# A decoder block's hand-ordered middle stretch rewritten: projection's second half to the FFN's second round

## The chip, the core and the metric

The kernel runs on one core of one Trainium2 chip. The metric is the device time of one execution in microseconds (us), and the number compared is the median of several runs. PE is TensorE (matmul), DVE is VectorE, ACT is ScalarE, POOL is GpSimd, SP is SyncE. In this kernel SP issues the loads and POOL issues the stores of intermediate results.

## What is computed

One layer of a decoder block on a sequence of 1024 tokens, width D = 1024, all in float32. A mixer (a gated convolution and a stick-breaking attention, merged) is projected back by `w_o`, normalised, gated and added to x. Then comes a SwiGLU feed-forward network (FFN) of inner width D_FF = 2816, with RMSNorm before and after and shift, scale and gate from the conditioning vector c:

```python
def swiglu_ffn(h, w_ffn_in, w_ffn_out):
    gate, up = jnp.split(h @ w_ffn_in, 2, axis=-1)
    return (jax.nn.silu(gate) * up) @ w_ffn_out
...
        h = rmsnorm(x, pre_mix_g[l]) * (1.0 + sc1) + sh1
        y = hybrid_mixer(h, w_in[l], conv_w[l], ...)        # ends in merged @ w_o
        x = x + ga1 * rmsnorm(y, post_mix_g[l])
        h = rmsnorm(x, pre_ffn_g[l]) * (1.0 + sc2) + sh2
        y = swiglu_ffn(h, w_ffn_in[l], w_ffn_out[l])
        x = x + ga2 * rmsnorm(y, post_ffn_g[l])
```

The change lies between `merged @ w_o` and the first rounds of `h @ w_ffn_in`.

## The kernel before, in words

**Layout.** Channels lie on the 128 partitions, tokens run along the free axis in two halves c = 0 and c = 1 of 512. A float32 product is made of three fp32r passes: each operand is split into `hi` (a copy rounded to fp32r, on ACT) and `lo` (the difference, on DVE), and PE adds hi·hi, hi·lo and lo·hi in one PSUM bank. One matmul is 128x512 by 128x128. A weight tile of 128x1024 is loaded as `raw` and then split (`load_w`); raw, hi and lo have three buffers each in the pool `wp`.

**Projection.** `merged @ w_o` makes eight output tiles of 128 channels for each token half, 24 matmuls each (8 input tiles, 3 passes). The second half (c = 1) is `step(k)`, in the order `WORDER`. Three of its weights are still in their buffers from the first half; five are loaded and split again. `evac` copies a bank out on ACT, squares it on ACT and adds the square into `ysum` on DVE. `total` sums `ysum` over channels with a matmul by `ones` in plain fp32 (banks `psq`, `psx`). `res` multiplies by the root from that sum, adds x and squares the sum on ACT; a second total (`psx`) gives the pre-FFN norm, and `scaled` applies it: a DVE multiply by the root, then ACT's scale and shift.

**FFN, first matmul.** It runs in 22 rounds f, one per block of 128 gate and 128 up channels. Each round computes its four half-blocks (gate and up, two token halves) with a scheme of seven products instead of eight, each of 4 x 3 = 12 matmuls. The operands on the token side are B11, B21 (parts of the first token half), T1 to T4 (sums of parts of both halves) and B22. The weight side of a round needs the sums s1 to s4 and the parts a11, a12 and a22. The products accumulate in the banks `ka`, `kc` and `kb`. The first two products of a round need only the first token half, so for the first `EARLY` = 9 rounds they are done ahead (`ke(f, 0)` and `ke(f, 1)`, with weight `early_w(f)`), beside the second half's norms. Each goes to a bank of its own; ACT copies the first out (`e_first`), DVE adds the second to it (`e_second`), and both results are stored to DRAM in `e_d` and loaded again in round f. So a round f < EARLY has 60 matmuls and a later one 84.

**FFN, second matmul.** Its weight is used in the same scheme. `w2_forms(j)` makes its sums during rounds 9 to 19 (`W2_AT`, which follows `EARLY`), 4 stores of 512 KB each into `w_d`. The gated results go to `g_d` through POOL and are loaded as X and Y. `gb11_0` is the first operand of this matmul, made on ACT from X.

**Order.** `pin(begin)` fixes the order in which instructions stand on PE, DVE and ACT from `begin` (before `step(0)`) to the last early product, as the code is written. Everything else, and all of SP and POOL, is ordered by the scheduler. An instruction waits for its inputs and for a free buffer, and all behind it on its engine wait with it. The lines that matter most:

```python
        def early_w(f):
            wes[f] = load_w(w1[f], f"we{f}", act, dve)
...
        for j in (2, 3):
            los.append(operand("T2", j, t2s[j]))
        early_w(6)
        ke(5, 0)
        ke(5, 1)
```

## Time and profile before

| | |
|---|---|
| median of 3 runs | 1459.28 us (1458.99 to 1460.12) |
| the profiled execution's own time | 1457.92 us |
| its span, first to last instruction | 1456.1 us |
| PE busy | 1389.9 us (95% of the span) |
| DVE busy | 1021.7 us (70%) |
| ACT busy | 658.6 us (45%) |
| mean granted TensorE clock | 0.993 |

The median is what a change is measured by. The rows further down come from the profiled execution, whose span lies 1.8 us below its own time. Busy shares are averages over stages with different limits, so what an edit is worth is read from the stage that it touches. In a list of waits each row names the engine and the tile that it wrote, whom it waited for, the sum, the number of waits and the longest.

### The profile page before, as it was taken

Reading aid. Unit: us, or ns where it says so; the run is one execution under the profiler, and the core shown is the slowest. Engines: PE = TensorE matmul, PEld = TensorE weight load, DVE = VectorE, ACT = ScalarE, POOL = GpSimd, SP = SyncE. Lnnn points to the kernel's source line nnn. Section 1 sums busy time; section 2 is a strip of 40 time slices with the busy share of each in tenths; the row PEclk is TensorE's granted clock in tenths of the full one; section 3 lists DMA queues with packets and bytes.
Section 4 is the critical chain, followed back from the end, with each engine's and each line's share of the span. In section 5 each row is a group of like instructions: output and inputs, shape, how many; then the busy total and the mean of one; then the engine's idle time right before and its main releaser. Section 6 shows DMA issues by size and latency. Waiting matters only on the chain.

```text
span 1456.1 us, 18905 instructions
## 1 busy us (share of the span) xinstructions
PE 1389.9 (95%) x6888; PEld 1162.5 (80%) x6888; DVE 1021.7 (70%) x1503; ACT 658.6 (45%) x1143; POOL 193.2 (13%) x275
## 2 busy tenths in 40 slices
PE   5999999999999999999989899999999997999996
...
GB/s 380 84 44 68 122 44 145 50 61 95 44 131 117 248 141 206 274 249 143 284 116 149 126 180 163 134 174 252 254 253 246 253 191 358 116 318 296 285 120 116
DMA packets 89932, 255.84 MB, mean 176 GB/s; under 512 B 9584, under 2 KB 19952, under 8 KB 88816
## 3 DMA queue, kind: packets, MB, share of 16 engines
...
## 4 chain that ended last, share of the span: by engine, by line
issue 46%; PE 43%; POOL 6%; DMA 2%; DVE 2%; ACT 1%; POOLq 0%; SPq 0%; DVEq 0%; ACTq 0%
PE ka L1222 8%; PE pb L1222 4%; PE pg L179 3%; PE pgv L179 3%; PE pv L381 3%; PE pcv L361 3%; PE pgg L179 2%; PE pq L179 2%; PE pk L179 2%; PE pa L1222 2%; PE tr L471 2%; POOL w_d L106 2%; POOL g_d L106 2%; PE av L481 1%; PE av L480 1%
## 5 line engine op out<-in xcount | busy, mean ns | idle before, releaser
L461 POOL TENSOR_TENSOR be<-be,ka 128x127 f32<-128x127 f32 (+2 forms) x96 | 99.8, 1053 | 233.7 <-DVE ka L459 118.5
L459 DVE TENSOR_TENSOR_SCAN ka<-ka 128x128 f32<-128x128 f32 (+2 forms) x96 | 95.2, 1015 | 40.1 <-ACT ka L455 40.0
L475 DVE TENSOR_TENSOR alo<-tr,ahi 128x512 fp32r<-128x512 f32 x80 | 53.3, 684 | 44.2 <-ACT ahi L474 43.7
L455 ACT ACTIVATE ka<-z 128x128 f32<-128x128 f32 (+2 forms) x96 | 47.7, 498 | 54.9 <-PE z L454 36.3
L474 ACT ACTIVATE ahi<-tr 128x512 fp32r<-128x512 f32 x80 | 46.5, 603 | 44.9 <-PE tr L471 32.5
L1222 PE MATMUL ka<-gt,w2f 128*128 128x512 f32 x264 | 63.1, 389 | 0.0
L1222 PEld LDWEIGHTS ka<-gt,w2f 128*128 128x128 f32 x264 | 49.6, 188 | 10.3
L790 PE MATMUL pwo<-mhi,wo_hi 128*128 128x512 f32 x128 | 51.0, 398 | 3.4 <-ACT wo_hi L158 1.7
L955 PE MATMUL ke<-b,we_hi 128*128 128x512 f32 x144 | 47.8, 414 | 5.3 <-ACT we_hi L158 5.3
L134 DVE SCALAR_TENSOR_TENSOR ada<-ada,cb 128x1024 f32<-128x1024 f32 x32 | 39.0, 1222 | 17.5 <-DMA ada<-in_ada_dram 17.3
L790 PE MATMUL pwo<-mhi,wo_lo 128*128 128x512 f32 x128 | 50.0, 390 | 0.5 <-DVE wo_lo L168 0.5
L456 ACT ACTIVATE be<-z 128x128 f32<-128x128 f32 (+2 forms) x96 | 47.4, 502 | 6.0 <-PE tr L471 5.9
L790 PE MATMUL pwo<-mlo,wo_hi 128*128 128x512 f32 x128 | 50.0, 390 | 0.1
L471 PE MATMUL tr<-ident,be 128*128 128x128 f32 x288 | 49.2, 273 | 0.7 <-DVE alo L475 0.4
L480 PE MATMUL av<-ahi,vst 128*128 128x256 f32 x160 | 44.6, 293 | 2.0 <-ACT be L456 1.2
L481 PE MATMUL av<-alo,vst 128*128 128x256 f32 x160 | 43.2, 296 | 2.1 <-DVE alo L475 1.9
L106 POOL DMA_DIRECT2D g_d<-uw x22 | 11.9, 543 | 246.2 <-DVE uw L1175 246.2
L361 PE MATMUL pcv<-ph,cvw 128*128 128x128 f32 x320 | 42.8, 276 | 1.3 <-DMA ph<-v_d 1.3
L361 PEld LDWEIGHTS pcv<-ph,cvw 128*128 128x128 f32 x320 | 39.7, 192 | 2.1 <-DMA ph<-v_d 1.1
L1103 PE MATMUL kb<-b,a 128*128 128x512 f32 x156 | 40.9, 389 | 0.0
L1222 PE MATMUL ka<-gb,wa 128*128 128x512 f32 x132 | 33.2, 400 | 7.9 <-ACT gb L158 7.9
L1103 PE MATMUL ka<-b,a 128*128 128x512 f32 x156 | 39.7, 389 | 0.0
(512 smaller groups left out, 4075.6 us busy)
## 6 DMA issues: line engine op xcount, KB each, us to landing
...
w2r<-in_w_dram SPq DMA_DIRECT2D x44, 256.0 KB, 3.8
...
```

Of the source, the lines that this page charges most:

```text
L106: nc.gpsimd.dma_start(dst, src)
L179: pe.matmul(bank, st[:, cols], mv[k][:, c * CH:(c + 1) * CH], start=(i == 0 and s == 0), stop=(i == n - 1 and s == 2))
L361: pe.matmul(cv[:, gi * TM:(gi + 1) * TM], wts[n][:, at:at + P], ph[:, g, SH - 1 - d:SH - 1 - d + TM], start=(d == 0), stop=(d == SH - 1))
L459: dve.tensor_tensor_scan(rev, rev, rev, init, op0=ALU.mult, op1=ALU.bypass)
L461: pool.tensor_tensor(beta[:, :m], beta[:, :m], kap[:, s_lo + 1:s_lo + 1 + m], op=ALU.mult)
L471: pe.transpose(tr[:, o:o + P], src, ident)
L475: dve.tensor_tensor(alo, tr, ahi, op=ALU.subtract)
L480: pe.matmul(avc, lhs, ahi[:, cols], start=(jp == c and jj == 0), stop=False)
L481: pe.matmul(avc, lhs, alo[:, cols], start=False, stop=(jp == 0 and jj == 1))
L790: pe.matmul(bank_, st[:, cols], mv[k][:, cs], start=(k == 0 and q == 0), stop=(k == KT - 1 and q == 2))
L1103: pe.matmul(bank_, st[:, cols], t[:, mv], start=(first and j == 0 and s == 0), stop=(j == HK - 1 and s == 2), skip_group_check=not first)
L1222: pe.matmul(dst, w[st][:, cols], g[mv], start=first and s == 0, stop=last and s == 2, skip_group_check=more)
```

## The change

It rewrites the hand order from the projection's second half on and lets it run on through rounds 0 and 1 of the FFN (`PIN = 2`). For this, `ffn(f)` is a generator that yields between its products, so that the hand order can put other instructions between them. `evac` is cut into its ACT and its DVE part, `load_w` into load (`wl`), hi (`wh`) and lo (`wlo`), and a root into its ACT part and a function for its DVE part. EARLY goes from 9 to 11. Both early products of a block accumulate in one bank; ACT copies it out after the first and after the second, and DVE adds nothing. They are done in twos: `ke(4,0)`, `ke(5,0)`, `ke(4,1)`, `ke(5,1)`. The norm is one DVE operation (times scale, times root), and the shift is added where hi and lo are made, or in the sums T1 to T4. psx1 sums five tiles instead of eight. The sums of round 0 have three tiles of their own.

```diff
-EARLY = 9
+EARLY = 11
...
-        def scaled(c, n, r):
-            y = h2[n, c]
-            dve.tensor_tensor(y, y, r, op=ALU.mult)
-            act.activation(y, y, AF.Identity, bias=mod[:, 24 + n:25 + n], scale=scale2[:, n:n + 1])
...
-        def make_b(n, eng):
-            t, y = B_AT[n], h2[n, 0]
-            copy_to(eng, t[:, 0], y)
-            dve.tensor_tensor(t[:, 1], y, t[:, 0], op=ALU.subtract)
...
-        def e_first(f):
-            es[f] = wtmp(f"e0_{f}")
-            act.activation(es[f], kbs[f, 0], AF.Copy)
-            store(e_d[f][:, 0], es[f])
-
-        def e_second(f):
-            e1 = wtmp(f"e1_{f}")
-            dve.tensor_tensor(e1, kbs[f, 1], es[f], op=ALU.add)
-            store(e_d[f][:, 1], e1)
-
-        def t2_sub(j):
-            b11, b12, b22 = h2[j, 0], h2[j, 1], h2[HK + j, 1]
-            dve.tensor_tensor(b11, b12, b11, op=ALU.subtract)
-            t2 = t2s[j] = wtmp(f"t2_{j}")
-            dve.tensor_tensor(t2, b22, b11, op=ALU.subtract)
...
+        def norm(c, n, r):
+            y = h2[n, c]
+            dve.scalar_tensor_tensor(y, y, scale2[:, n:n + 1], r, op0=ALU.mult, op1=ALU.mult)
+
+        def shift(n):
+            return mod[:, 24 + n:25 + n]
+
+        def bh(t, n, c):
+            act.activation(t[:, 0], h2[n, c], AF.Identity, bias=shift(n), scale=1.0)
+
+        def bl(t, n, c):
+            dve.scalar_tensor_tensor(t[:, 1], h2[n, c], shift(n), t[:, 0], op0=ALU.add, op1=ALU.subtract)
...
+        def ke(f, i):
+            if i == 0:
+                kbs[f] = dbank(f"ke{f}")
...
+                    pe.matmul(kbs[f], wes[f][st][:, cols], t[:, mv], start=(i == 0 and j == 0 and q == 0),
+                              stop=(j == HK - 1 and q == 2), skip_group_check=i > 0)
+
+        def e(f, i):
+            t = wtmp(f"e{i}_{f}")
+            act.activation(t, kbs[f], AF.Copy)
+            store(e_d[f][:, i], t)
...
+        def t12(j):
+            b11, b12, b22 = h2[j, 0], h2[j, 1], h2[HK + j, 1]
+            dve.tensor_tensor(b11, b12, b11, op=ALU.subtract)
+            T2[j] = wtmp(f"t2_{j}")
+            dve.scalar_tensor_tensor(T2[j], b22, shift(HK + j), b11, op0=ALU.add, op1=ALU.subtract)
+            hi_of("T2", j, T2[j])
...
+        for i, t in enumerate((xsum, xs(1, 2), xs(1, 6), xs(1, 3), xs(1, 7))):
+            pe.matmul(psx, ones, t, start=i == 0, stop=i == 4)
...
+        s0 = [po_.tile([P, CH], F32, tag="wt", name=f"s0_{i}", bufs=3) for i in range(3)]
+        for t, src in zip(s0, (w1[0][:, :CH], w1[FT][:, :CH], w1[FT][:, CH:])):
+            load(t, src)
...
+        for _ in r1:
+            pass
+        pin(begin)
+
+        for f in range(PIN, FT):
+            raw_w(f)
+            for _ in ffn(f):
+                pass
```

Three places show how instructions move. In the rows an arrow points from what is read to what is written.

The first place is ACT in the projection's second half. Squares of the residual sum are `xr0_*<-y0_*`; `y1_*<-pwo1_*` and `ysq1_*<-pwo1_*` are the copy and the square of an output tile; `wo1_3_hi` and `wo1_2_hi` are hi halves of the fifth and sixth weight. Before:

```order
L827 ACTIVATE xr0_4_6366<-y0_0_6199 128x512
L827 ACTIVATE xr0_4_6366<-y0_1_6234 128x512
L798 ACTIVATE y1_2_6608<-pwo1_6_6536,gpost1_159 128x512
L804 ACTIVATE ysq1_6_6610<-pwo1_6_6536 128x512
L827 ACTIVATE xr0_6_6369<-y0_2_6276 128x512
L827 ACTIVATE xr0_6_6369<-y0_3_6318 128x512
L158 ACTIVATE wo1_3_hi_6623<-wo1_3_raw_6621 128x1024
L798 ACTIVATE y1_3_6655<-pwo1_7_6583,gpost1_159 128x512
L804 ACTIVATE ysq1_7_6657<-pwo1_7_6583 128x512
L158 ACTIVATE wo1_2_hi_6667<-wo1_2_raw_6665 128x1024
```

After, where `w_o4_hi` and `w_o5_hi` are the hi halves of the same two weights and `L834` has the squares:

```order
L834 ACTIVATE xr0_2_6365<-y0_2_6278 128x512
L798 ACTIVATE y1_2_6590<-pwo1_1_6565,gpost1_159 128x512
L804 ACTIVATE ysq1_6_6592<-pwo1_1_6565 128x512
L158 ACTIVATE w_o4_hi_6594<-w_o4_raw_6499 128x1024
L834 ACTIVATE xr0_2_6365<-y0_3_6320 128x512
L834 ACTIVATE xr0_4_6368<-y0_0_6201 128x512
L834 ACTIVATE xr0_4_6368<-y0_1_6236 128x512
L798 ACTIVATE y1_3_6641<-pwo1_2_6616,gpost1_159 128x512
L804 ACTIVATE ysq1_7_6643<-pwo1_2_6616 128x512
L158 ACTIVATE w_o5_hi_6645<-w_o5_raw_6501 128x1024
```

Before, all eight squares of the residual, up to `xr0_6`, stand ahead of the fifth weight's hi; after, three of them do (`xr0_0` twice, `xr0_2` once), the next three follow it, and `xr0_6` comes behind the sixth.

The second place is ACT around the seventh early weight (`we6_hi` before, `w_6_hi` after). `L840` is the scale and shift of the second token half, `T2_*o` are hi halves of T2, `e0_*` and `e1_*` copies out of an early product's bank. Before:

```order
L158 ACTIVATE we5_hi_7087<-we5_raw_7085 128x1024
L960 ACTIVATE e0_4_7117<-ke4_0_7091 128x512
L840 ACTIVATE y1_2_6608<-y1_2_6608,mod_156,scale2_158 128x512 x2
L840 ACTIVATE y1_3_6655<-y1_3_6655,mod_156,scale2_158 128x512 x2
L976 ACTIVATE T2_0o_7134<-t2_0_7125 128x512
L976 ACTIVATE T2_1o_7145<-t2_1_7132 128x512
L976 ACTIVATE T2_2o_7150<-t2_2_7143 128x512
L976 ACTIVATE T2_3o_7152<-t2_3_7148 128x512
L158 ACTIVATE we6_hi_7156<-we6_raw_7154 128x1024
L960 ACTIVATE e0_5_7186<-ke5_0_7160 128x512
```

After:

```order
L158 ACTIVATE w_5_hi_7076<-w_5_raw_6900 128x1024
L980 ACTIVATE e1_3_7091<-ke3_7018 128x512
L158 ACTIVATE w_6_hi_7094<-w_6_raw_6975 128x1024
L980 ACTIVATE e0_4_7118<-ke4_7078 128x512
L980 ACTIVATE e0_5_7134<-ke5_7121 128x512
L985 ACTIVATE T2_0o_7140<-t2_0_7138 128x512
L158 ACTIVATE w_7_hi_7156<-w_7_raw_7054 128x1024
L985 ACTIVATE T2_1o_7161<-t2_1_7159 128x512
L980 ACTIVATE e1_4_7163<-ke4_7078 128x512
L158 ACTIVATE w_8_hi_7184<-w_8_raw_7098 128x1024
```

The hi of weight 6 stood behind four scale-and-shift instructions (two rows with x2) and four of T2, and now stands behind one copy-out after the hi of weight 5; `L840` is gone, and the T2 rows alternate with the weights 7 and 8.

The third place is the start of the second FFN matmul, on ACT and on POOL, whose stores signal in turn on the semaphores DMASW0 to DMASW7. `wa*` are weights of the second matmul, `gb11_0` its first operand. ACT before:

```order
L158 ACTIVATE wa11_2_10448<-wa_2_10367 128x512 [waits DMAHW4_49,DVE_49,PE_49]
L1174 ACTIVATE uw_21_10192<-uw_21_10192 128x512 [waits DVE_49]
L158 ACTIVATE wa12_2_10454<-wa_2_10367 128x512 [waits PE_49]
L158 ACTIVATE gb11_0_10373<-X0_10330 128x512 [waits DMASW7_49,DVE_49]
L158 ACTIVATE gb21_0_10379<-X0_10330 128x512 [waits DMASW1_49]
L158 ACTIVATE gb11_1_10412<-X1_10331 128x512 [waits DMAHW5_49,DMASW2_49]
```

ACT after:

```order
L158 ACTIVATE wa11_2_10442<-wa_2_10361 128x512 [waits DMAHW2_49,DVE_49,PE_49]
L1287 ACTIVATE uw_21_10158<-uw_21_10158 128x512 [waits DVE_49]
L158 ACTIVATE wa12_2_10448<-wa_2_10361 128x512 [waits PE_49]
L158 ACTIVATE gb11_0_10367<-X0_10324 128x512 [waits DMAHW3_49,DMASW1_49,Activation_49]
L158 ACTIVATE gb21_0_10373<-X0_10324 128x512 [waits DMASW5_49]
L158 ACTIVATE gb11_1_10406<-X1_10325 128x512 [waits DMAHW4_49,DMASW2_49,DVE_49]
```

POOL's last stores before:

```order
L106 DMA w_d10_132<-w2o_10_2_10043 128x1024 [waits DMASW0_49,DVE_49]
L106 DMA w_d10_132<-w2o_10_3_10048 128x1024 [waits DMASW1_49,DVE_49]
L106 DMA g_d8_119<-uw_19_9898 128x512 [waits DMASW2_49,DVE_49]
L106 DMA g_d8_119<-p1_19_9897 128x512 [waits DMASW3_49,DVE_49]
L106 DMA g_d9_120<-uw_20_10059 128x512 [waits DMASW4_49,DVE_49]
L106 DMA g_d9_120<-p1_20_10058 128x512 [waits DMASW5_49,DVE_49]
L106 DMA g_d10_121<-uw_21_10192 128x512 [waits DMASW6_49,DVE_49]
L106 DMA g_d10_121<-p1_21_10191 128x512 [waits DMASW7_49,DVE_49]
```

POOL's last stores after:

```order
L106 DMA g_d9_120<-uw_20_9997 128x512 [waits DMASW4_49,DVE_49]
L106 DMA g_d9_120<-p1_20_9996 128x512 [waits DMASW5_49,DVE_49]
L106 DMA w_d10_132<-w2o_10_1_10293 128x1024 [waits DMASW6_49,DVE_49]
L106 DMA w_d10_132<-w2o_10_0_10298 128x1024 [waits DMASW7_49,DVE_49]
L106 DMA w_d10_132<-w2o_10_2_10303 128x1024 [waits DMASW0_49,DVE_49]
L106 DMA w_d10_132<-w2o_10_3_10308 128x1024 [waits DMASW1_49,DVE_49]
L106 DMA g_d10_121<-uw_21_10158 128x512 [waits DMASW2_49,DVE_49]
L106 DMA g_d10_121<-p1_21_10157 128x512 [waits DMASW3_49,DVE_49]
```

Before, `gb11_0` waits for a signal on DMASW7, which is that of the last row, `g_d10<-p1_21`. After, it waits for DMASW1, which is that of `w_d10<-w2o_10_3`; the four `w_d10` stores moved from ahead of round 19's `g_d8` stores to between the stores of rounds 20 and 21.

## Rows read from the trace of the kernel before

**Rows 1.** The windows of core 0; busy us, (x) instructions, granted clock, DMA share, GB/s.

```profile
core 0: us, PE busy (x) PEld busy (x) DVE busy (x) ACT busy (x) POOL busy (x), PEclk, DMA share, GB/s
724.88:862.02 137.14, 121.57 (x492) 92.81 (x490) 109.76 (x166) 77.13 (x119) 18.35 (x34) 0.98 0.40 134
740.00:785.00 45.00, 38.14 (x159) 29.31 (x159) 37.77 (x56) 28.11 (x43) 3.24 (x6) 1.00 0.40 127
862.02:1217.66 355.64, 355.64 (x1571) 294.48 (x1569) 266.72 (x425) 145.92 (x256) 46.29 (x86) 1.00 0.64 219
1205.00:1235.00 30.00, 22.06 (x89) 17.78 (x88) 15.91 (x25) 9.88 (x17) 1.62 (x3) 0.89 1.03 390
```

**Rows 2.** PE's waits over the span, longest in total first.

```profile
engine line waited for: us in total, times, longest us
...
PE ka L1222 <- ACT gb L158: 7.9, 1, 7.9
PE ke L955 <- ACT we_hi L158: 5.3, 1, 5.3
...
PE psq L809 <- DVE ysum L805: 2.2, 1, 2.2
...
PE pwo L790 <- ACT wo_hi L158: 1.7, 1, 1.7
PE kc L1103 <- ACT s4o L158: 1.6, 1, 1.6
PE psx L809 <- DVE xsum L907: 1.5, 1, 1.5
```

**Rows 3.** PE's timeline around psx1 and from 825 us: start, duration, instruction.

```profile
start us, us, engine line op out<-in xcount [idle before <-releaser]
795.66 3.59 PE L999 MATMUL psx<-xr,ones 128*128 128x512 f32 x8
798.70 1.03 PE L955 MATMUL ke<-b,we_hi 128*128 128x512 f32 x2
799.56 0.39 PE L955 MATMUL ke<-b,we_lo 128*128 128x512 f32 x1
...
825.52 1.22 PE L955 MATMUL ke<-b,we_hi 128*128 128x512 f32 x2 [5.34 <-ACT we_hi L158]
...
831.21 0.42 PE L955 MATMUL ke<-b,we_hi 128*128 128x512 f32 x1
```

**Rows 4.** DVE's timeline: lows of weights and operands, and the tail's norm and adds.

```profile
829.65 1.21 DVE L168 TENSOR_TENSOR we_lo<-we_raw,we_hi 128x1024 fp32r<-128x1024 f32 x1
830.78 0.68 DVE L978 TENSOR_TENSOR T_0o<-y,T_0o 128x512 fp32r<-128x512 f32 x1
...
1422.85 0.69 DVE L154 SCALAR_TENSOR_TENSOR frs<-frs10a,frs 128x512 f32<-128x512 f32 x1
1423.57 5.39 DVE L1362 SCALAR_TENSOR_TENSOR yc<-yc,gpost,frs 128x512 f32<-128x512 f32 x8
1428.88 4.90 DVE L1262 TENSOR_TENSOR yc<-yc,xr 128x512 f32<-128x512 f32 x8
```

**Rows 5.** ACT's timeline: a copy out of PSUM, then two hi halves of weights.

```profile
795.51 0.58 ACT L960 ACTIVATE e<-ke 128x512 f32<-128x512 f32 x1
795.99 1.99 ACT L158 ACTIVATE we_hi<-we_raw 128x1024 fp32r<-128x1024 f32 x2
```

**Rows 6.** PE's timeline from round 21 into the second FFN matmul.

```profile
1217.66 0.84 PE L1103 MATMUL ka<-T_3o,a 128*128 128x512 f32 x3
1226.44 2.08 PE L1222 MATMUL ka<-gb,wa 128*128 128x512 f32 x4 [7.94 <-ACT gb L158]
...
1233.05 1.98 PE L1222 MATMUL pa<-gb,wa 128*128 128x512 f32 x8
```

**Rows 7.** ACT's and POOL's timeline ahead of the second FFN matmul.

```profile
1225.76 2.71 ACT L158 ACTIVATE gb<-X 128x512 fp32r<-128x512 f32 x5 [6.59 <-DMA g_d<-p]
...
1219.52 0.54 POOL L106 DMA_DIRECT2D g_d<-p  x1 [0.79 <-DVE p L1182]
```

**Rows 8.** DMA issues in 1120 to 1170 us.

```profile
issues: line engine op xcount, KB each, median us to landing
...
g_d<-p POOLq DMA_DIRECT2D x3, 256.0 KB, 2.9
```

**Rows 9.** DMA issues in 1215 to 1230 us.

```profile
g_d<-p POOLq DMA_DIRECT2D x1, 256.0 KB, 6.2
```

More of the change, by code (lines that the diff above doesn't have):

```diff
@@ new lines, in tile_block, with m, a @@
+        for k in (3, 4, 5):
+            wl(W(k), wo[WORDER[k]])
+        evac_a(0, KT - 1, yb)
+        evac_d(0, KT - 1)
+        S(0, 0, 4)
+        psq = total("psq0", ysum[0])
+        S(0, 4)
+        fin = root("yrs0", psq)
+        ya(0)
+        wh(W(3))
+        r = fin()
+        def m(n):
+            dve.tensor_tensor(h2[n, 0], h2[n, 0], r, op=ALU.mult)
+        def a(n):
+            res_add(0, n)
+        m(0)
+        m(1)
+        a(0)
+        m(2)
+        a(1)
+        wlo(W(3))
@@ new lines, in tile_block @@
+        wl(0, w1[0])
+        xadd(0, xsum, 5, 6, 7)
+        S(3)
+        ya(3)
+        wh(W(6))
+        S(4, 0, 6)
+        psx = total("psx0", xsum)
+        S(4, 6)
+        fin = root("xrs0", psx)
+        xr_load(1)
+        wlo(W(6))
+        wl(1, w1[1])
+        yd(2)
+        yd(3)
+        r = fin()
+        wh(W(7))
+        for n in range(4):
+            norm(0, n, r)
+            b0h(n)
+        wlo(W(7))
+        wl(2, w1[2])
+        S(5)
+        ya(4)
+        wh(0)
+        norm(0, 4, r)
@@ new lines, in tile_block @@
+        norm(0, 5, r)
+        b0l(0, 1)
+        norm(0, 6, r)
+        norm(0, 7, r)
+        b0h(4, 5, 6, 7)
+        b0l(2, 3)
+        wlo(0)
+        wl(3, w1[3])
+        S(6)
+        ya(5)
+        yd(4)
+        yd(5)
+        b0l(4, 5, 6, 7)
+        ya(6)
+        wh(1)
+        yd(6)
+        S(7)
+        ke(0, 0)
+        ya(7)
+        wlo(1)
+        wl(4, w1[4])
+        yd(7)
+        wh(2)
+        e(0, 0)
+        wlo(2)
+        wl(5, w1[5])
+        psq = total("psq1", ysum[1])
@@ new lines, in tile_block, with m, a @@
+        ke(1, 0)
+        fin = root("yrs1", psq)
+        ke(0, 1)
+        e(1, 0)
+        e(0, 1)
+        wh(3)
+        r = fin()
+        def m(n):
+            dve.tensor_tensor(h2[n, 1], h2[n, 1], r, op=ALU.mult)
+        def a(n):
+            res_add(1, n)
+        ke(1, 1)
+        m(0)
+        m(4)
+        a(0)
+        m(1)
+        a(4)
+        e(1, 1)
+        wlo(3)
+        m(5)
+        a(1)
+        wl(6, w1[6])
+        ke(2, 0)
+        xsum = wtmp("xsum1")
+        dve.tensor_tensor(xsum, xs(1, 0), xs(1, 4), op=ALU.add)
@@ L1127, in tile_block, with ffn @@
+        def ffn(f):
             if f:
[L1128 to L1129 removed]
+                a11, a12, a21, a22 = raws.pop(f)
+            else:
+                (s2, s3, s1), (a12, a22) = s0, raws.pop(f)
             def bk(nm):
```

500 lines of the change are left out of this document (272 added, 228 removed).

## The prediction

> **What bounds the kernel now.** I read the windows first. TensorE (PE) is busy for nearly the whole span, and in 862.02 to 1217.66 without a gap: 355.64 us busy of 355.64, granted clock 1.00 [rows 1]. In that stretch 1569 matmuls start (8 rounds of 60 and 13 of 84, less the last three, which start at 1217.66 [rows 6]), so a 128x512 matmul takes 355.64 / 1569 = 0.2267 us. Such a stretch gains nothing from shorter work on DVE or ACT; a gain needs a place where PE waits or runs slowly. The list of PE's waits [rows 2] names those places. Leaving the start and the attention aside, they are the wait of 7.9 us before the second FFN matmul, one of 5.3 us in the early products, and several of 1.5 to 2.2 us, all of these shorter ones between 724.88 (the first matmul of the projection's second half) and 862.02 (the end of round f=0). That stretch is what the change rewrites.
>
> It lasts 137.14 us [rows 1]. Its matmuls are 8 x 24 of the projection, 18 early half-products of 12, and 60 of round 0, in all 468, or 106.10 us. Its sums over channels (psq, psx) are fp32 ones-matmuls, of which each runs as two passes: psx1's eight come in two groups of four, and one group shows as x8, holds PE from 795.66 to 798.70 and makes the next two matmuls last 0.86 us where two take 0.45 [rows 3], in all 3.45 us, or 0.431 a pass. With one matmul each for psq0, psx0 and psq1 the stretch has 11, or 22 passes: 9.48 us. PE's count of 492 [rows 1] is 468, these 22 and two at the border. What is left is 137.14 - 106.10 - 9.48 = **21.56 us of waits and slow clock**. It is made up of the 5.34 us wait with what refills PE after it, then 12 matmuls from 825.52 to 831.21, 5.69 us where 2.72 are due [rows 3], so 2.97 lost to the clock, and some 13 us of shorter waits.
>
> **The change, part by part.** *PE.* Of the eight ones-matmuls of psx1, five stay, because DVE adds four squares beforehand. Three matmuls, or six passes, go: **2.58 us**. Two more blocks get their early products, 4 x 12 matmuls that later rounds no longer do, so the number of matmuls is unchanged. The after-kernel's pinned stretch holds 192 + 22 x 12 + 2 x 60 = 576 matmuls (130.58 us) and 16 passes (6.90 us), or 137.48 us without waits: from 724.88 to 862.36.
>
> *Projection half.* In the before-kernel the hi halves of the last weights stand behind ACT's squares of the residual, which wait for DVE; hence the 1.7 us on wo_hi and 1.5 on xsum [rows 2]. In the new order each hi goes ahead of the squares, and the raw weight was loaded long before. Stepping through the new order with the intervals of [rows 4, 5] (DVE: an add 0.61 us, a fused norm 0.664, 0.72 from start to start where it needs the one before it, lo of a weight 1.13; ACT: hi 0.94, as the last 0.1 of a row overlaps the next, copy out of PSUM 0.48), the hi of the fourth to sixth outputs are done some 9, 9 and 8 us before PE needs them, and the sums for psx0 and psq1 are done 0.2 to 0.5 us before PE arrives. So I take 0 there; a slip of each by one DVE operation costs about 1.3 us in all.
>
> *Early products.* The 5.34 us wait is for the hi of weight 6, which stands on ACT behind four shifts, four T2 copies and a copy-out, and these wait for DVE. Now ACT has no shift to do (the norm is one DVE operation), and hi of weight 6 stands right after hi of 5. After psx1 (ending at 794.35) the DVE chain is lo(5) at 798.1, three sums of round 0 at 800.1, the root's three dependent operations at 802.35, lo(6) 1.13, six norms (5.31 / 8 each [rows 4]) 3.98, two T1/T2 pairs at 1.44, lo(7) 1.13: **811.5**. PE, without a wait, is at 797.07 after 288 matmuls and 16 passes; it needs lo(7) at its third matmul of that product, 811.1, so it waits 0.4. In the same way lo(8) costs 1.2, and lo(9), whose buffer comes free only when block 6's products end, 0.85. What is late next is DVE itself: it now carries the norms, the lows of nine weights and sixteen operands, and PE catches up with it at these points. The nine DVE adds of block sums that go (0.6 each) are in the chain as zero; the ACT copies that replace them (13 more at 0.48) lie beside PE's 2.72 us products. If ACT were the late one instead, three such copies ahead of a hi would cost 1.4.
>
> *Rounds 0 and 1.* These follow the pins too. Where PE waited 1.6 us for s4o [rows 2], I find, in the same stepping, 0.7 (s4o of round 0, behind four lows of B22), 1.15 (a22, behind T4), 1.15 and 0.2 (s1o and s3o of round 1, behind seven DVE operations). **Waits left: 0.4 + 1.2 + 0.85 + 0.05 + 0.7 + 1.15 + 1.15 + 0.2 = 5.7 us**, so round 1 ends at 862.36 + 5.7 = 868.1. In the before-kernel round 1 ends after the same 576 matmuls at 862.02 + 108 x 0.2267 = 886.5. **The difference is 18.4 us.** Bounds: no wait left, 24.1; twice as much, 12.6. None of the waits is above the ones which in 740 to 785 (6.9 us of PE's 45 idle, with the 2.2, 1.7 and 1.5 waits in it) left the granted clock at 1.00 [rows 1], so the 2.97 us of slow clock go with the 5.34 us wait.
>
> *Rounds 2 to 21.* They hold the same work per round of either kind; PE never waited there. EARLY = 11 puts the W2 sums two rounds later, into f=11 to 21, where each still meets a round of 84 matmuls, 19.0 us. I take 0.
>
> *Transition.* There PE stops at about 1218.5, waits 7.94 us for gb and then does 20 matmuls in 6.61 us where 4.53 are due (1226.44 to 1233.05 [rows 6]). gb stands on ACT until 1225.76, released by the store g_d<-p, which POOL issued at 1219.52 [rows 7]. The store needed 6.2 us in that stretch [rows 9] and 2.9 in 1120 to 1170 [rows 8]; the DMA engines are full (1.03, 390 GB/s [rows 1]). Now gb waits instead for the last of the four w_d stores of round 21 (the two orders above). It depends on DVE's lo of that form, which has no fixed place ahead of round 21's end; by the intervals of DVE it is issued 6 to 2 us before the round's last matmul, and with 6 to 10 us in the crowd it lands 0 to 8 us behind it; today gb comes 1225.76 - 1218.5 = 7.3 us after the products. As four such stores of twice the size follow each other, I take the late end, a change of 0. If it opens when only the products are done (about 1.2 us after the last matmul), 6.7 us of the wait and the 2.08 of slow clock go: +8.8. If the 2 MB of stores run in full into the saturated stretch, 2.1 MB / 390 GB/s = 5.4 us are lost: -5.4.
>
> The Trainium skill (DMA: Bandwidth & Descriptors, section "Issuing engines are not separate DMA queues") says that transfers issued by different engines still run on the same 16 DMA engines and interleave. The trace agrees: the same 256 KB store took 2.9 us before and 6.2 in the crowd. By that rule the moved stores slow the loads of X, Y and wa, which speaks against this part of the change; by it the sum is that of rival 2, and with separate queues it would be the 0 taken.
>
> **The sum.** 21.56 + 2.58 - 5.7 + 0 = 18.4 us. The profiled execution took 1457.92 (its span 1456.1), so 1439.5; the median of the three runs is 1.36 above the profiled one, so **1440.9**, which I round to 1441.0.
>
> **Rivals.**
> 1. *The transition opens early*: the w_d store lands before the products end. For it: round 21's stores then go out one by one, and gb11_0 no longer waits for the last store of all. Against it: four 512 KB stores are queued ahead of it. Gain 18.4 + up to 8.8: 1432 to 1437.
> 2. *The transition closes later by the 2 MB*: 18.4 - 5.4 = 13.0, 1446.3. For it the full DMA engines; against it that the w_d loads and stores began before the stretch.
> 3. *DVE gives half back.* DVE is busy for 110 of the 137 us [rows 1], and every wait left above is on it; of its 166 operations there some 60 lie on the path, and 0.1 us more on each takes 6 us, and a load late for the three added tiles makes it 9 to 12: gain 6 to 9, 1450 to 1453. From 18.4 - 2.9 = 15.5 us on no gain could be told.
> 4. *It doesn't do what it says*: the waits only move, since the data they stand for (root, norms, T operands) is ready no sooner. For it: DVE, on which they all depend, has hardly fewer operations to do. Against it: 5.34 + 2.97 us came from an ACT queue that no longer holds what was waited for. Within 2.9 us of 1459.3.
> 5. *Slower.* From 811 to 868 PE has eight short waits in a row. If the clock fell to its lower level at the first and stayed there, as it did after the 5.34 us wait (0.474 us a matmul, 0.247 above the 0.2267 [rows 3]), some 228 matmuls would cost 56 us: 1497. It ends the gain at 18.4 / 0.247 = 74 slow matmuls. Against it the 1.00 in 740 to 785 [rows 1], with four waits.
>
> The Trainium skill (TensorE: Matmul & The Clock Gate, section "A second HAM failure mode: psum-queue depth-cycling") tells of a kernel whose frequent short idles between groups of matmuls sent the clock back and forth between its two levels. That would be rival 5; the trace shows no case of it with waits of this size.
>
> **How the numbers follow.** A measurement of this kernel can tell about 0.2%, 2.9 us, from no change. Chances: the forecast (gain 14 to 23) 0.55; rival 1 0.17; rival 2 0.15; rival 3 0.08; rival 4 0.03; rival 5 0.02. The range takes in rivals 1 and 2 and the two bounds of the waits (24.1 and 12.6, which give 1435.2 and 1446.7), and at its upper end the near side of rival 3: 1432 to 1449. Faster: 0.55 + 0.17 + 0.15 + 0.08 = 0.95; same 0.03; slower 0.02.
>
> **What would show it.** Right: the wait on hi of weight 6 gone; no PE wait over 1.5 us from the projection's second half to the end of round 1; a granted clock of 1.00 there; round 1 ending about 868 (counted so that the projection's second half starts at 724.88); psx1 as five ones-matmuls that take 10 x 0.431 = 4.3 us; then no wait until the second FFN matmul, and there one of 7 to 8 us that ends with a w_d store. Wrong: waits on DVE (lo of 7, 8, 9) above 2 us; a clock below 1.00; a wait of a quite different length at the transition, or PE waits in rounds 19 to 21, where the W2 sums now lie.

## The result and the profile after

The changed kernel takes 1439.64 us (median of 4 runs, 1438.42 to 1440.23), against 1459.13 us for the kernel before in the runs beside it. The ratio is 0.9869, with an interval of 0.9852 to 0.9886: faster by 1.3%, or 19.5 us by the medians. The forecast was 1441.0.

The two profiled spans differ by 1456.1 - 1438.2 = 17.9 us. To see where, I cut both at four places: the first matmul of the projection's second half (psq0's row less the 12 matmuls ahead of it: 724.88 before, 726.19 - 2.72 = 723.47 after), the last three matmuls of round 21, the first matmul on gb, and the end of the span.

| stretch, us | before | after | won |
|---|---|---|---|
| up to the projection's second half | 724.88 | 723.47 | 1.41 |
| from there to round 21's last three matmuls | 492.78 | 476.62 | 16.16 |
| from there to the first matmul on gb | 8.78 | 7.60 | 1.18 |
| from there to the end | 229.66 | 230.51 | -0.85 |

The change does not rewrite the first stretch, and over the profiles of all kernels shown here it ends between 720.92 and 726.50. So 1.41 us there lie within its scatter, and I count them as no part of the change.

PE's waits in the rewritten stretch, 730 to 868, of the changed kernel (line, what waited for what, sum, number, longest):

```profile
engine line waited for: us in total, times, longest us
PE ke L975 <- DVE w_lo L909: 1.4, 2, 0.8
PE ka L867 <- DVE uw L1282: 0.9, 1, 0.9
PE kc L867 <- DVE s1o L858: 0.8, 1, 0.8
PE kc L867 <- DVE uw L1267: 0.7, 1, 0.7
PE ka L867 <- DVE uw L1267: 0.2, 1, 0.2
```

In the kernel before the same list had 5.3, 2.2, 1.7, 1.6 and 1.5 at its head [rows 2]. Now five lines remain, each below 1 us at its longest, 4.0 us in all, and none lies in the projection's second half or in the early products ahead of weight 8. The rows themselves show where the rest is:

```profile
814.06 0.50 PE L975 MATMUL ke<-b,w_lo 128*128 128x512 f32 x1 [0.84 <-DVE w_lo L909]
...
823.10 0.50 PE L975 MATMUL ke<-b,w_lo 128*128 128x512 f32 x1 [0.52 <-DVE w_lo L909]
...
845.42 0.70 PE L867 MATMUL kc<-B_0o,s4o 128*128 128x512 f32 x2 [0.68 <-DVE uw L1267]
...
849.33 0.70 PE L867 MATMUL ka<-T_0o,a 128*128 128x512 f32 x2 [0.91 <-DVE uw L1282]
...
856.35 0.50 PE L867 MATMUL kc<-T_0o,s1o 128*128 128x512 f32 x1 [0.84 <-DVE s1o L858]
...
859.12 0.70 PE L867 MATMUL ka<-T_0o,s3o 128*128 128x512 f32 x2 [0.17 <-DVE uw L1267]
...
867.42 0.62 PE L867 MATMUL ka<-T_0o,s2o 128*128 128x512 f32 x2
```

These are the lows of weights 8 and 9, the two points of round 0 (s4o, a22) and the two of round 1 (s1o, s3o) that the prediction named, with 0.84, 0.52, 0.68, 0.91, 0.84 and 0.17 us. Round 2 begins at 867.42. The windows of the changed kernel (as in [rows 1]):

```profile
723.47:867.42 143.95, 139.96 (x593) 110.36 (x592) 119.09 (x174) 82.77 (x129) 21.52 (x40) 1.00 0.46 154
867.42:1200.09 332.67, 331.80 (x1463) 274.06 (x1462) 256.98 (x409) 135.97 (x239) 45.19 (x84) 1.00 0.65 221
740.00:785.00 45.00, 44.96 (x195) 36.10 (x194) 42.35 (x62) 29.57 (x45) 6.39 (x12) 1.00 0.46 149
```

The rewritten stretch runs at a granted clock of 1.00 throughout, where the kernel before had 0.98 [rows 1], and 740 to 785, where PE was idle for 6.9 us, is now full. The second row, rounds 2 to 21, has 0.9 us in which PE is idle; before it had none. That is one new wait, and a second new one lies in the second FFN matmul:

```profile
1031.31 0.73 PE L867 MATMUL ka<-T_0o,a 128*128 128x512 f32 x2 [0.75 <-DVE uw L1282]
...
1289.30 0.70 PE L1397 MATMUL ka<-gt,w2f 128*128 128x512 f32 x2 [0.65 <-DMA w2f<-w_d]
```

The ones-matmuls of psx1 are five, ten passes, 4.31 us from 789.05 to 793.36 (the 0.41 by which the matmuls behind them are late counted in):

```profile
789.05 1.02 PE L1163 MATMUL psx<-xsum,ones 128*128 128x512 f32 x2
789.91 3.59 PE L1163 MATMUL psx<-xr,ones 128*128 128x512 f32 x8
792.95 1.03 PE L975 MATMUL ke<-b,w_hi 128*128 128x512 f32 x2
```

At the start of the second FFN matmul PE, ACT and POOL show:

```profile
1200.09 0.84 PE L867 MATMUL ka<-T_3o,a 128*128 128x512 f32 x3
1207.69 2.08 PE L1397 MATMUL ka<-gb,wa 128*128 128x512 f32 x4 [6.76 <-ACT gb L158]
...
1214.10 1.98 PE L1397 MATMUL pa<-gb,wa 128*128 128x512 f32 x8
...
1207.01 2.71 ACT L158 ACTIVATE gb<-X 128x512 fp32r<-128x512 f32 x5 [5.41 <-DMA w_d<-w2o]
...
1192.82 2.34 POOL L106 DMA_DIRECT2D w_d<-w2o  x4 [4.16 <-DVE w2o L878]
```

gb, which waited for g_d<-p before [rows 7], now waits for w_d<-w2o; ACT begins it at 1207.01, and the first matmul on it starts at 1207.69, 7.60 us after the last three matmuls of round 21 start, where it was 8.78. The next 20 matmuls take 6.41 us where they took 6.61.

### The profile page after: what moved, and what is told of

Its sections match the earlier page's. It is cut to its first block, busy times and chain, and to the rows that moved or that the text cites. A ratio compares the mean times of both kernels' runs of the same rounds, so it can differ in the third digit from the quotient of the medians.

```text
span 1438.2 us, 18913 instructions
## 1 busy us (share of the span) xinstructions
PE 1384.5 (96%) x6882; PEld 1159.7 (81%) x6882; DVE 1020.9 (71%) x1496; ACT 653.8 (45%) x1136; POOL 195.4 (14%) x279
## 3 DMA queue, kind: packets, MB, share of 16 engines
q0 software_dynamic: 15936, 54.54, 10.1%
## 4 chain that ended last, share of the span: by engine, by line
PE 52%; issue 26%; DMA 7%; DVE 7%; POOL 4%; ACT 2%; SPq 0%; POOLq 0%; DVEq 0%; ACTq 0%
PE ka L1397 8%; PE pwo L790 6%; PE pb L1397 4%; PE pg L179 3%; PE pgv L179 3%; PE pv L381 3%; PE pcv L361 3%; PE pgg L179 2%; PE pq L179 2%; PE pk L179 2%; PE pa L1397 2%; PE tr L471 2%; PE ka L315 2%; POOL w_d L106 2%; POOL g_d L106 2%
## 5 line engine op out<-in xcount | busy, mean ns | idle before, releaser
L975 PE MATMUL ke<-b,w_hi 128*128 128x512 f32 x176 | 55.1, 394 | 0.0
L975 PEld LDWEIGHTS ke<-b,w_hi 128*128 128x128 f32 x176 | 33.0, 188 | 7.7 <-issue 1.0
L381 PE MATMUL pv<-wv_hi,hhi 128*128 128x256 f32 x128 | 37.1, 290 | 1.4 <-DVE qst L405 0.8
L158 ACT ACTIVATE gt<-X 128x512 fp32r<-128x512 f32 x33 | 20.4, 629 | 38.9 <-PE ka L1397 11.6
L471 PEld LDWEIGHTS tr<-ident,be 128*128 128x128 f32 x288 | 35.0, 140 | 2.6 <-POOL be L461 1.1
L381 PE MATMUL pv<-wv_hi,hlo 128*128 128x256 f32 x128 | 36.5, 285 | 0.0
```

The lines of the kernel that those rows point to most:

```text
L381: pe.matmul(pv[:, :256], st[k][:, tcols], mv[:, wc], start=(k == 0 and i == 0), stop=(k == KT - 1 and i == 2))
L471: pe.transpose(tr[:, o:o + P], src, ident)
L975: pe.matmul(kbs[f], wes[f][st][:, cols], t[:, mv], start=(i == 0 and j == 0 and q == 0), stop=(j == HK - 1 and q == 2), skip_group_check=i ...
```

## The experiments

Besides the medians I give for each profile two lengths that other stretches don't disturb: **A**, from the projection's second half to the T3 product of round 1 (135.65 us in the changed kernel), and **B**, from the projection's second half to round 21's last three matmuls (476.62; before 492.78). A kernel with fewer early products is set level by 0.2267 us for each matmul that comes later.

**Are three of the parts needed?** First EARLY back to 9, with the W2 sums back in rounds 9 to 19 with it.

```diff
-EARLY = 11
+EARLY = 9
...
-        wl(9, w1[9])
...
-        ke(10, 1)
-        e(10, 1)
```

> The changed kernel with EARLY = 9: the early products of blocks 9 and 10 go back into their rounds, all else of the hand order stays, and the W2 sums go back with EARLY. Theory: the two blocks are cover for DVE's chain. PE reaches round 0's fourth product 48 x 0.227 = 10.9 us sooner, DVE only 2 x 1.13 us sooner, so PE waits 6 to 9 us more in the stretch from weight 8 to the end of round 1, perhaps with a low clock behind one of the waits (2 to 3 us): the stretch loses 6 to 12 us. Rival, that the order alone made the gain: it loses under 2 us. At the second FFN matmul the buffers wait for other stores (gb11_0 for one of round 19, gb21_0 for one of round 21), so 0 to 7 us come back there; the stages are read apart.

Measured: 1441.72 us, ratio 0.989 (0.9873 to 0.9906). A is 128.06, or 138.94 with the 48 matmuls, 3.3 us longer; B is 478.42, 1.8 longer. PE's waits from 800 to 860, the two longest lines:

```profile
PE kc L867 <- DVE uw L1265: 2.2, 1, 2.2
PE ka L867 <- DVE uw L1265: 1.3, 2, 1.1
```

PE does come earlier to round 0 and waits more for DVE there (2.2 and 1.1 where it was 0.7 and nothing), at a clock of 1.00. But the theory had 6 to 12 us: the two blocks' own work on ACT and DVE goes as well, and the waits that remained were in that place already. Half of the 3.3 us comes back in the rounds, since the new wait of rounds 2 to 21 is gone. At the second FFN matmul gb11_0 comes at once and the second operand waits 4.0 us instead.

Then psx1 with eight ones-matmuls.

```diff
-        for i, t in enumerate((xsum, xs(1, 2), xs(1, 6), xs(1, 3), xs(1, 7))):
-            pe.matmul(psx, ones, t, start=i == 0, stop=i == 4)
+        for i, n in enumerate((0, 4, 1, 5, 2, 6, 3, 7)):
+            pe.matmul(psx, ones, xs(1, n), start=i == 0, stop=i == 7)
```

> The changed kernel with psx1 as eight ones-matmuls instead of five (and without the four DVE sums ahead of it). Theory: the three matmuls lie on PE's path, 6 x 0.431 = 2.6 us slower, partly hidden where PE waits for DVE's lows of weights 8 and 9 (1.4 us) which then start sooner: 1.2 to 2.6 us slower in the stretch. Rival, that PE's later waits for DVE absorb all of it: under 0.5 us.

Measured: 1440.23 us, ratio 0.9887 (0.9872 to 0.9901). A is 138.22, 2.57 us longer: the full price, nothing of it hidden, and the waits behind it are the same to 0.05 us. B is only 1.1 longer, because the wait in rounds 2 to 21 is absent in this profile; by the medians the kernels can't be told apart.

The norm and shift as before, in the new order:

```diff
-            dve.scalar_tensor_tensor(y, y, scale2[:, n:n + 1], r, op0=ALU.mult, op1=ALU.mult)
+            dve.tensor_tensor(y, y, r, op=ALU.mult)
+            act.activation(y, y, AF.Identity, bias=shift(n), scale=scale2[:, n:n + 1])
...
-            dve.scalar_tensor_tensor(T2[j], b22, shift(HK + j), b11, op0=ALU.add, op1=ALU.subtract)
+            dve.tensor_tensor(T2[j], b22, b11, op=ALU.subtract)
```

> The changed kernel, its hand order kept, with the norm and shift as before: DVE multiplies by the root, ACT does scale and shift in place, hi and lo are plain copies and differences, T1 to T4 plain differences. DVE has as many operations as in the changed kernel, ACT 16 more of 0.7 us. Theory that the fusion matters because ACT's part lies between DVE's norm and what DVE needs next: each of the four T1/T2 pairs waits 0.7 to 1 us for ACT, DVE falls behind by 3 to 4 us around the lows of weights 7 to 9, and PE waits that much more; the first token half has slack: 3 to 5 us slower, 1442 to 1445. Rival, that the order alone made the gain and ACT's slack hides it: under 1 us.

Measured: 1448.08 us, ratio 0.9923 (0.9898 to 0.9948); A 143.86, 8.2 us longer, twice what was expected. Not the lows are late but a sum and a copy, and the clock falls behind both (windows as in [rows 1]):

```profile
775.99 2.07 PE L816 MATMUL psq<-ysum,ones 128*128 128x512 f32 x2 [2.83 <-DVE ysum L808]
...
810.67 1.22 PE L976 MATMUL ke<-b,w_hi 128*128 128x512 f32 x2 [3.27 <-ACT e L981]
...
770.50 0.69 DVE L808 TENSOR_TENSOR ysum<-ysum,ysq 128x512 f32<-128x512 f32 x1 [4.12 <-ACT ysq L804]
```

```profile
774.00:786.00 12.00, 10.01 (x36) 7.54 (x37) 8.59 (x13) 4.76 (x8) 2.12 (x4) 0.86 0.42 133
808.00:822.00 14.00, 11.33 (x38) 9.11 (x39) 10.93 (x16) 9.99 (x16) 2.12 (x4) 0.76 0.40 128
```

The first wait, on psq1, comes from the first token half, for which I had expected slack: on ACT the square of an output tile stands behind eight shifts and eight copies, and DVE, which is to add it, stands idle for 4.12 us (third row) with all that follows. Behind that wait the 12 us from 774 on have a clock of 0.86, behind the second (a copy-out that stands on ACT behind shifts) the 14 us from 808 on 0.76.

**Do they add up?** All three undone together; what stays is the hand order, twos, one bank.

```diff
-EARLY = 11
+EARLY = 9
...
+            act.activation(y, y, AF.Identity, bias=shift(n), scale=scale2[:, n:n + 1])
...
+        for i, n in enumerate((0, 4, 1, 5, 2, 6, 3, 7)):
+            pe.matmul(psx, ones, xs(1, n), start=i == 0, stop=i == 7)
```

> The changed kernel with three of its parts undone together: the shift on ACT, eight ones-matmuls in psx1, EARLY = 9. What stays is the hand order, early products in twos into one bank, and the order of rounds 0 and 1. Up to the end of round 1 the three cost 8.2, 2.6 and 3.3 us when undone alone, together 14.1 of the 18.4 won there. If they add up, the stretch is 4 us shorter than in the kernel before, 1453 to 1456. Rival, that they overlap (each one undone alone leaves PE to wait at the same DVE chain): 8 to 11 us shorter than before, 1446 to 1450. If they need each other: slower than before.

Measured: 1449.37 us, ratio 0.995 (0.9931 to 0.9969). A is 138.39, or 149.27 set level, 13.6 us longer than in the changed kernel, where the sum of the three is 14.1. B is 488.77, 4.0 us shorter than before. By this profile they nearly add up in the stretch, and the order with twos and one bank by itself is worth 4 us of the 16. By the medians they don't: 1449.37 is 8.7 us below the kernel before beside it (4.5 to 10.1 by the interval), which is the rival's range. The profiled run, at 1453.96, was the slowest of the five, 4.6 us above the median. So what the order is worth by itself lies between 4 and 10 us, and whether the parts add up or overlap is not settled.

**One part alone in the kernel before.** First only weight 6 sooner on ACT:

```diff
         e_first(4)
+        early_w(6)
         scaled(1, 2, r)
...
-        early_w(6)
         ke(5, 0)
```

> The kernel before with one edit: weight 6 is split right after the copy-out of block 4, ahead of four scale-and-shift operations and four T2 copies on ACT. Theory that the 5.34 us wait and the 2.97 us of slow clock behind it are ACT's order alone: the wait falls to under 1.5 us, the clock in that stretch is 1.00, 6 to 8 us faster than before, of which up to 2 us come back at the next lows, as DVE's lo of weight 6 moves ahead of its norms. Rival, that the data (DVE's norms) are late and the wait moves to the next weight: under 3 us faster.

Measured: 1458.53 us, ratio 0.9998 (0.9985 to 1.001), B 492.75 where it was 492.78. Its waits:

```profile
PE ke L955 <- ACT we_hi L158: 3.9, 1, 3.9
PE ke L955 <- DVE we_lo L168: 2.8, 3, 1.3
```

The wait on a hi is 3.9 instead of 5.3 and comes one block of 24 matmuls later, at weight 7, and that on lows has grown from 1.5 to 2.8. The rival was right: the wait moves to the next weight. Its hi stands on ACT behind the T2 and T1 copies, of which those of T2 wait for DVE's norms and sums.

Then only the fused norm and shift, in the old order:

```diff
-            dve.tensor_tensor(y, y, r, op=ALU.mult)
-            act.activation(y, y, AF.Identity, bias=mod[:, 24 + n:25 + n], scale=scale2[:, n:n + 1])
+            dve.scalar_tensor_tensor(y, y, scale2[:, n:n + 1], r, op0=ALU.mult, op1=ALU.mult)
...
-            dve.tensor_tensor(t2, b22, b11, op=ALU.subtract)
+            dve.scalar_tensor_tensor(t2, b22, shift(HK + j), b11, op0=ALU.add, op1=ALU.subtract)
```

> The kernel before, its order kept, with the fused norm and the shift in hi, lo and the sums T1 to T4 as in the changed kernel: ACT has 16 operations of 0.7 us fewer, DVE as many as before. Theory that the 5.34 us wait and the slow clock behind it come from DVE's chain being slowed by ACT's shifts (moving weight 6 alone won nothing): 5 to 9 us faster, the wait on the hi of weight 6 under 2 us, the waits of the projection half (1.70, 0.53, 1.51, 0.93, 2.19) as before. Rival, that the fusion only pays in the new order: under 3 us.

Measured: 1457.08 us, ratio 0.9996 (0.9987 to 1.0005), B 492.18. The wait on weight 6's hi is still 4.4 us:

```profile
779.62 0.84 PE L809 MATMUL psq<-ysum,ones 128*128 128x512 f32 x1 [2.06 <-DVE ysum L805]
...
823.63 0.73 PE L963 MATMUL ke<-b,we_hi 128*128 128x512 f32 x2 [4.40 <-ACT we_hi L158]
```

The rival again: what is worth 8.2 us in the new order is worth 0.6 in the old one. In this profile the clock fell to 0.66 in 780 to 785, behind the wait on psq, where the kernel before kept 1.00, so 0.6 is a low figure; by the interval of the medians it is 1.9 us at most.

Why it pays in one order and not in the other can be read from where ACT begins the second root (xrs1) and where DVE makes the last T2 sum. In this order: the kernel before, this run, the new order with the shift on ACT, the changed kernel:

```profile
805.48 0.69 ACT L150 ACTIVATE xrs1r<-psx,eps 128x512 f32<-128x512 f32 x1 [7.51 <-PE psx L999]
805.66 0.69 ACT L150 ACTIVATE xrs1r<-psx,eps 128x512 f32<-128x512 f32 x1 [8.57 <-PE psx L1007]
799.26 0.69 ACT L928 ACTIVATE xrs1r<-psx,eps 128x512 f32<-128x512 f32 x1 [2.31 <-PE psx L1164]
793.55 0.69 ACT L928 ACTIVATE xrs1r<-psx,eps 128x512 f32<-128x512 f32 x1 [2.27 <-PE psx L1163]
...
823.16 0.69 DVE L972 TENSOR_TENSOR t<-y,y 128x512 f32<-128x512 f32 x1
821.16 0.75 DVE L980 SCALAR_TENSOR_TENSOR t<-y,mod,y 128x512 f32<-128x512 f32 x1
824.04 0.69 DVE L996 TENSOR_TENSOR t<-y,y 128x512 f32<-128x512 f32 x1
814.64 0.75 DVE L995 SCALAR_TENSOR_TENSOR t<-y,mod,y 128x512 f32<-128x512 f32 x1
```

Counted from the start of the projection's second half, the root begins at 80.6, 80.9, 74.6 and 70.1 us, and the last T2 sum at 98.3, 96.4, 99.4 and 91.2. In the old order the fusion brings the T2 sums 1.9 us sooner but the root no sooner, for the waits ahead of it stay (2.06 us on psq where it was 2.19). In the new order it brings the root 4.5 us sooner, with the 2.83 us wait on psq gone, and the T2 sums 8.2 us.

**What the one bank costs.** Early products one block after the other:

```diff
         e(4, 0)
-        ke(5, 0)
-        e(5, 0)
+        ke(4, 1)
+        e(4, 1)
...
-        ke(4, 1)
+        ke(5, 0)
```

> The changed kernel with the two halves of an early block one behind the other on PE (4,0 4,1 5,0 5,1) instead of in twos; they share one bank, so the second half's first matmul waits until ACT has copied the first half's result out. Theory: each block then costs a wait of about 1 us (PE's drain, ACT's copy of 0.58 us, refill), for 11 blocks 8 to 12 us, of which up to 2 us lie in waits for DVE that then shrink: 6 to 11 us slower, clock 1.00. Rival, that the copy is hidden by PE's own pipeline: under 2 us.

Measured: 1449.68 us, ratio 0.9955 (0.9941 to 0.9969), A 147.00, 11.35 us longer. PE waits nine times for the copy-out:

```profile
799.29 0.72 PE L975 MATMUL ke<-b,w_hi 128*128 128x512 f32 x2 [0.74 <-ACT e L980]
...
808.55 0.79 PE L975 MATMUL ke<-b,w_hi 128*128 128x512 f32 x1 [3.51 <-ACT e L980]
```

Eight waits are 0.69 to 0.74 us, and the nine are 9.3 us in sum; what the 11.35 has above that is drain, refill and a lower clock, which the expectation (6 to 11 us at 1.00) left out. The one of 3.51 us is a copy-out that stands on ACT behind a T2 copy, which waits for DVE; the clock is 0.84 in 805 to 810 and 0.82 in the next 5 us. So here one bank for two halves is free only in twos.

**Rounds 0 and 1 by the scheduler.** `pin(begin)` moved to right behind the last early product.

```diff
         e(10, 1)
+        pin(begin)
         for j in range(HK):
             b22h(j)
...
-        pin(begin)
```

> The changed kernel with the hand order ending after the last early product, so that rounds 0 and 1 are ordered by the scheduler as in the kernel before. Four waits of rounds 0 and 1 (0.68, 0.91, 0.84 and 0.17 us) are what the hand order leaves there. If the hand order of the two rounds is part of the gain, PE waits 1.5 to 3 us more there, as before (1.6 for s4o and 1.2 for s1o): 1441 to 1443. Rival: the scheduler does as well, within 0.5 us in the stretch.

Measured: 1442.01 us, ratio 0.9888 (0.9871 to 0.9906). B is 475.61, 1.0 us shorter than in the changed kernel. So the hand order of these two rounds is no part of the gain. That the kernel is not faster comes from elsewhere: in this profile the stretch ahead of the change is 1.6 us longer, and that from round 21 to the end 1.25 us, as gb11_0 comes at once but the second operand waits 6.01 us.

**The wait at the second FFN matmul.** W2 sums back in rounds 9 to 19, with EARLY = 11:

```diff
-W2_AT = tuple(range(EARLY, EARLY + FH))
+W2_AT = tuple(range(9, 9 + FH))
```

> The changed kernel with the W2 sums back in rounds 9 to 19 (EARLY stays 11). The theory that the wait ahead of the second FFN matmul hangs on the last store that its first operand's buffer waits for: in this order gb11_0 waits for the store g_d8<-uw_19, two rounds old, and gb11_1 and gb21_0 for stores of round 20, so the 6.76 us wait falls to 1 to 2 us and the 1.9 us of slow clock behind it go: 1431 to 1434. The rival that the wait is for the saturated DMA engines in general (X0, wa or the queue): the wait stays at 5 to 8 us, 1438 to 1441. A third: DVE, with W2 sums in the short rounds 9 and 10 (60 matmuls), makes PE wait there; then 1 to 3 us are lost in those two rounds.

Measured: 1440.04 us, ratio 0.9878 (0.9859 to 0.9897). The wait falls to 1.24 us, as the theory had it, but the median does not, for the third case came as well, at more than its 1 to 3 us: B is 482.60, 6.0 us longer.

```profile
1002.36 1.06 PE L867 MATMUL ka<-T_0o,a 128*128 128x512 f32 x2 [4.14 <-DVE uw L1282]
...
1210.50 0.73 PE L1397 MATMUL ka<-gb,wa 128*128 128x512 f32 x2 [1.24 <-ACT gb L158]
...
999.80 0.69 DVE L881 TENSOR_TENSOR w2r<-w2r,w2r 128x512 f32<-128x512 f32 x1 [3.92 <-DMA w2r<-in_w_dram]
```

The first wait lies in the first rounds with W2 sums. On DVE a W2 sum stands until 999.80 for a load of w2r, and the sum that PE needs stands behind it; the DMA engines are busy 0.87 of 985 to 1002.

With rounds 10 to 20 instead:

```diff
-W2_AT = tuple(range(EARLY, EARLY + FH))
+W2_AT = tuple(range(10, 10 + FH))
```

> The changed kernel with the W2 sums in rounds 10 to 20. In the run with rounds 9 to 19 the wait ahead of the second FFN matmul fell to 1.24 us (7.3 us won there with the clock), but PE lost 6.0 us in the first rounds with W2 sums, which have 60 matmuls (13.6 us) and move some 5 MB each. Theory that a short round is too short for these transfers: with one short round instead of two, the loss is 1.5 to 3.5 us. The wait at the second matmul depends on which store gb11_0's buffer waits for: if that of round 19, the whole 7 us are won and the kernel is 3 to 5 us faster than the changed one, 1435 to 1437; if the last one of round 21, 0 to 2 us slower. Rival, that the loss in the rounds is DVE's own work: 5 to 6 us lost as in the other run.

Measured: 1444.35 us, ratio 0.9911 (0.9892 to 0.9931); B 476.83, 0.2 us longer than in the changed kernel: PE does not wait in the short round at all, so neither the 1.5 to 3.5 us of the theory nor the 5 to 6 of its rival came. PE waits 7.63 us for gb11_0, and the 20 matmuls behind take 7.30. By the order its buffer waits on DMASW3, the lane of round 21's last store; the profile names a load of Y as the last DMA ahead of it. That speaks for the wait hanging on where the buffer lies, and not on how early the W2 sums are done; the last run below tests it.

The loads of Y put behind those of X on SP, so that the stores have more room:

```diff
-            load(y, g_d[j][:, :, 1])
+            ins = nc.sync.dma_start(y, g_d[j][:, :, 1])
+            tc.add_manual_dep(ins.ins, lastx[0].ins.name, mybir.DependencyInfo(
+                mybir.DependencyClass.NoSync, mybir.DependencyReason.SCHED_ONLY))
```

> The changed kernel with the loads of Y put behind the last load of X on SP, so that they no longer run beside the w_d stores of round 21. Theory that the stores are late because of the crowd: the last w_d store, which took 12.3 us, takes 6 to 8, gb11_0 opens 4 to 6 us sooner and the slow clock behind it shrinks: 1433 to 1436. Rival, that the four stores in a row set the time themselves or X and wa fill the engines as well: under 1.5 us.

Measured: 1441.25 us, ratio 0.9879 (0.9855 to 0.9903). The first matmul on gb starts 7.62 us after the last three of round 21, as in the changed kernel (7.60). The DMA issues in 1185 to 1207 of this run show why:

```profile
DMA packets 3400, 8.92 MB, mean 406 GB/s; under 512 B 291, under 2 KB 291, under 8 KB 3398
...
wa<-in_w_dram SPq DMA_DIRECT2D x4, 512.0 KB, 11.5
X<-g_d SPq DMA_DIRECT2D x4, 512.0 KB, 14.4
w_d<-w2o POOLq DMA_DIRECT2D x4, 512.0 KB, 9.7
```

No Y is there, but four wa and four X are, and the engines move 406 GB/s all the same; the w_d stores take 9.7 us, where in the same window of the changed kernel they took 10.3. The rival was right.

Last, the same instructions in the same order (the two traces list the same ones on PE, DVE, ACT and POOL, one for one), with the operand buffers at another address:

```diff
+        c11 = out_tiles("c11", (x_tile, x_tile))
         b2 = sweep("pa", prep1, (True, True))
-        c11 = out_tiles("c11", (x_tile, x_tile))
```

> The changed kernel with one line moved: the tiles of c11 are named ahead of the first sweep of the second FFN matmul instead of behind it. Every engine has the same instructions in the same order; only the memory at which the operand buffers of that matmul lie is another, so that gb11_0 waits for the store of p1_20, gb21_0 for none, gb11_1 for the second w_d store of round 21, and the last store of all is waited for by gb11_2, which PE needs some 11 us later. Theory that the 6.76 us wait is only the reuse of memory whose store is late: gb11_0 is made as soon as PE's last product allows, 1.2 us of wait, no slow clock behind it (4.6 us for the first 20 matmuls instead of 6.41), 7 us faster: 1431 to 1434. Rival, that X0, wa or the DMA engines hold it up anyway: within 2 us of the changed kernel, 1438 to 1441.

Measured: **1434.65 us** (1430.28 to 1435.19), ratio 0.9829 (0.9814 to 0.9844), faster than both kernels.

```profile
1201.48 0.84 PE L867 MATMUL ka<-T_3o,a 128*128 128x512 f32 x3
1203.56 1.19 PE L1397 MATMUL ka<-gb,wa 128*128 128x512 f32 x4 [1.24 <-ACT gb L158]
...
1208.22 1.97 PE L1397 MATMUL pa<-gb,wa 128*128 128x512 f32 x8
1211.23 2.11 PE L1397 MATMUL ka<-gb,wa 128*128 128x512 f32 x8 [1.03 <-DVE gb L1383]
...
1209.88 0.69 DVE L1440 TENSOR_TENSOR X<-Y,X 128x512 f32<-128x512 f32 x1 [4.97 <-DMA Y<-g_d]
```

The wait is 1.24 us, the first 20 matmuls take 4.66 us, and B is 476.75: 2.08 + 4.66 where the changed kernel had 7.60 + 6.41. A wait of 1.03 us comes behind it, for an operand's lo that stands on DVE behind a difference of the second sweep, which waits 4.97 us for a load of Y (last row). The spans differ by 5.5 us, the medians by 5.0, for 7.3 won at the transition; the rest goes to that wait and to stretches outside the transition.

## Why the prediction was right, and where it was not

**The rewritten stretch.** Forecast from the projection's second half to the end of round 1: 137.48 + 5.7 = 143.2 us; measured 867.42 - 723.47 = 143.95. The DVE chain that the early products hang on came as stepped out: lo(7) was to be done at 811.5, which is 810.1 in the changed kernel's time, and DVE goes on to its next instruction at 810.07. The waits came where they were said to be, but for lo(7) with 0.4, which didn't come, and the 0.05 for which the prediction names no place. The idle times are 0.84 for 1.2, 0.52 for 0.85, 0.68 for 0.7, 0.91 for 1.15, 0.84 for 1.15 and 0.17 for 0.2, in sum 4.0 for 5.7. At three of the four places in rounds 0 and 1 PE waits until DVE has emptied the bank (uw), and not for the operand that was named; DVE is the late engine at all six. The stretch is still 143.95 - 137.48 = 6.5 us above its matmuls. An idle time leaves out PE's drain and refill: from 812.61 to 814.40 three matmuls take 1.79 us where 0.68 are due, 1.11 lost for an idle time of 0.84. If the six waits have 0.27 each, that is 1.6 of the 2.5 us; the last 0.9 were not traced. psx1 gave 2.57 in its own run, for 2.58. The 2.97 us of slow clock went.

**The reason given for the 5.34 us wait** was wrong as it stood: "5.34 + 2.97 us came from an ACT queue that no longer holds what was waited for". With weight 6 moved ahead of that queue alone, B stayed at 492.75; with the shifts taken off ACT alone, at 492.18. Neither edit pays alone. In the new order the fusion is worth 8.2 us, the two added blocks 3.3 and psx1 2.6; what is left for order, twos and one bank is 4.0 by the profile, up to 10 by the medians. What the answer to rival 4 lacked is that the data themselves come sooner: the root begins 80.6 - 70.1 = 10.5 us sooner in the stretch, as PE reaches psx1 without the waits of the projection half and does it in one go, and the last T2 sum comes 7.1 us sooner. No run moved psx1 by itself, and none had weight 6 sooner and the fusion together in the old order, so the share of each is a reading.

**Two terms taken as 0 were not.** Rounds 2 to 21: 332.67 us where 1461 matmuls take 331.2, so 1.5 lost, with a wait of 0.75 us in which DVE stood for a load of a W2 sum. And the rest of the second FFN matmul is 0.85 us longer with the 20 matmuls counted, with a wait of 0.65 on w2f<-w_d that was not there before. Against them stand 1.18 at the transition, for which 0 was taken between +8.8 and -5.4. In sum 18.4 - 0.8 - 1.5 + 1.2 - 0.85 is 16.5; the other 1.4 of the 17.9 us between the profiles lie ahead of the change. So that 1441.0 came within 1.4 us of the median is in part luck: the path was right, the terms missed were about 2 us against the forecast, and scatter outside the change went the other way.

**The rivals.** The clock held 1.00 through the short waits, so the slower case didn't come, nor the going to and fro between clock levels of which the Trainium skill tells (TensorE: Matmul & The Clock Gate, "A second HAM failure mode: psum-queue depth-cycling"): with six short waits from 814 to 860 the trace shows 1.00. DVE did not give half back: of the 18.4 us some 0.8 went in this stretch. The transition neither opened early nor closed later by the 2 MB. That moved stores share the 16 engines, as the Trainium skill has it (DMA: Bandwidth & Descriptors, "Issuing engines are not separate DMA queues"), agrees with the run that took Y away: the engines stayed full. But the wait there was not set by their share: with other addresses and the same instructions it fell to 1.24 us. The bound of +8.8 for an early opening was nearly right: against the kernel before, with 8.78 + 6.61 us, that run has 2.08 + 4.66, 8.65 less, before the 1.03.
